# Four of sixteen gate projections computed with the values by Strassen's scheme, in a hybrid decoder layer on one core

## The chip, the cores and the metric

The kernel runs on 1 core of one Trainium2 chip. The metric is the device time of one execution in microseconds; the median of three runs before is 1684.72 us (1683.79 to 1685.11). The engines of the core, as the profile names them: PE is TensorE (matmuls, into banks of PSUM), DVE is VectorE, ACT is ScalarE, POOL is GpSimd, SP issues most transfers. Each of them works through its own instructions strictly in the order in which the program has them; semaphores make one wait for another.

## The reference, cut to what matters

One layer, x of 1024 rows x 1024 columns in float32. The part that the change touches is the combined projection of the normalised x and the use of its last 2048 columns, the gates.

```python
h = rms_norm(x, pre_mix_g[l])
proj = h @ w_in[l]
qa, ka, va, qb, kb, vb, gates = jnp.split(proj, split_at, axis=-1)
...
oa = diff_attention(qa, ka, va, lam)          # attention A: 4 heads, two softmaxes each, causal
...
    o_g, lse_g = dilated_group(qb[:, :, g], kb[:, :, g], vb[:, :, g], window, dil)   # attention B
...
g_a, g_b = jnp.split(jax.nn.sigmoid(gates), 2, axis=-1)
mix = (g_a * ya + g_b * yb) @ w_mix_out[l]
x = x + rms_norm(mix, post_mix_g[l])
```

After it comes a gated MLP with a convolution of three taps.

## The kernel before, in words

Every float32 product is made of three matmuls in a reduced format: each operand is split into a high part (a copy on ScalarE) and a rest (a subtraction on VectorE, L146), and `mm3` (L155 to L157) multiplies high by high, rest by high and high by rest. A matmul takes 128 x 128 weights and up to 512 moving columns. The stages are:

- **Values.** The 2048 value columns (512 of A, 1536 of B) are h times w_v. They are computed by Strassen's scheme on 2 x 2 blocks of 512: rows in two halves, the contraction in two halves of four 128-blocks, columns in halves. Seven products p1 to p7 replace eight; x enters as b11, b12, b21, b22 and the sums t2, t3, t4, the weights as blocks or sums of blocks. `steps_v` lists the steps in order, (product, column pair 0 or 1, k). `fetch_v` loads a step's weights 8 to 10 steps ahead, `ready_v` sums and splits them 5 steps ahead, `step_v` issues its 12 matmuls, and at a product's last k `take_v` moves the result from PSUM into the tiles y of the four quarters. The stores of the first columns' quarters, the norms of x, the angles and sines of the rotation are hung on step numbers (`STORE_AT`, `NORM_AT`, `TABLES_AT` and so on).
- **Attention A.** Four heads, each with eight blocks of 128 queries in the order 6, 7, 4, 5, 2, 3, 0, 1 (`attend_a`): scores (L784, L785) into two banks of PSUM, reduction with mask on VectorE (L787), exponentials on ScalarE (L794), ratio and combination of the two softmaxes on VectorE (L799 to L801); then, due one or two blocks later, transposes on TensorE (L713), split copies, products with the values (L725, L727), sums (L825, L826) and a norm by head (L857 to L866).
- **Attention B.** Twelve heads in three dilated groups, in the same manner with one softmax (`attend_b`).
- Merge, output projections with the gates, mix, up projection, down projection.

What fills TensorE beside the attention is projections: `proj_t` computes 128 columns for 1024 rows, 2 x 24 matmuls into one of three banks `acc`. A query or key projection is read from its bank by a rotation on ScalarE and VectorE (L700 to L703), a gate by one multiplication with the rows' norms (L250), after which it goes to a DRAM buffer `gt_d`. `interleave` spreads these fillers over the attention's steps by weight; `A_FILLS` gives them by head: p the next head's queries and keys (two projections), g a gate, v the transfer of the second pair of A's values, w their split, P, x and V the projections, transfer and value split of the first head of B. The framework then orders each engine's instructions by priority and readiness in a timeline of its own, so that fillers also move forward to where TensorE would stand; the position in the code doesn't settle the order.

Of the kernel before, what the change touches and what calls it, by code (L numbers as in the profile page):

```python
# [46 lines left out]
NH = NF // 2  # L47
AHEAD, T1_AT, LAST = 4, 5, 7
MIX_UNITS = {3: (0,), 4: (1,), 5: (2, 4), 6: (5,), 7: (6, 3, 7)}
START_GATES, A_FILLS, B_GATES = 1, ("gpgg", "gpvgg", "wgpgg", "xgPVgg"), 3  # L50
SLOTS = 18
LEFT_PAD = 48


XT_BUFS, NORM_AT, ANGLES_AT, SINES_AT, TABLES_AT, STORE_AT = 6, 14, 25, 33, 34, {35: 0, 36: 3, 39: 2, 41: 1}

K_FIRST = (4, 0, 5, 1, 6, 2, 7, 3)
RSQRT_MAGIC = float(0x5F3759DF)
# [29 lines left out]
def trunk(ctx: ExitStack, tc: tile.TileContext, a, out):  # L88
# [372 lines left out]
    with ExitStack() as st_y:  # L461
# [6 lines left out]
        def turns(pattern, *ps):  # L468

            ks = [iter(range(4)) for _ in ps]  # L470
            return [(ps[c], 1, next(ks[c])) for c in pattern]

        steps_v += [("p1", 1, k) for k in range(4)] + turns((0, 0, 1, 0, 1, 0, 1, 1), "p5", "p6")
        steps_v += turns((0, 0, 1, 1, 1, 1, 0, 0), "p3", "p7") + [("p4", 1, k) for k in range(4)]
        wz = [t[:, k % 2] for t in [wv.tile([P, 2, 512], F32, tag=f"wz{i}", name="wz") for i in range(2)] for k in range(2)]
        ready, got_v = {}, {}
# [10 lines left out]
        def new_y(name, pool=None):  # L487
            return [(pool or yv).tile([P, 512], F32, tag=f"y{name}{m}", name="yv") for m in range(4)]

        def fetch_v(n):  # L490
            p, i, k = steps_v[n]
            which = {"p1": ((0, 0),), "p2": ((0, 1),), "p5": ((1, 0), (1, 1)), "p6": ((0, 0),), "p7": ((0, 0), (1, 0)),
                     "p4": ((1, 1),), "p3": ((0, 1),)}[p]
            got_v[n] = [load_raw(a["w_v"][j * 4 + k][:, (2 * i + c) * 512 : (2 * i + c + 1) * 512], next(tags), parts=1 if n else 2)
                        for c, j in which]

        def ready_v(n, w=512):
            p, _, k = steps_v[n]
# [54 lines left out]
        quarter = {(0, i): new_y(f"a{i}") for i in range(2)}  # L553
        banks = {}

        def step_v(n):
            p, i, k = steps_v[n]
            x = xs_of[p]
            if p in ("p1", "p2", "p5") and k == 0:
                left = p == "p1"  # L560
                banks[left] = ([psum() for _ in range(3)] + [psum(F32, ps_o, "o")] if left else
                               [psum(F32, q, t) for q, t in ((ps_s, "s"), (pt, "pt")) for _ in range(2)])
            use = banks[p in ("p1", "p6", "p7", "p4")]
            wh, wl = ready.pop(n)
            for m in range(4):
                tk = slice(m * P, (m + 1) * P)
                mm3(use[m], x[0][:, k, tk], x[1][:, k, tk], wh, wl, k == 0 and p in ("p1", "p2", "p5"), k == 3, p in ("p6", "p7", "p4", "p3"))
            if k < 3:
                return
            with tc.high_priority(offset=80):  # L570
                for m in range(4):
                    take_v(p, i, m, use[m])
            if p == "p7" and i == 0:
                for m in range(4):
                    tt(quarter[3, 0][m], banks[False][m], quarter[3, 0][m], ALU.add)
# [56 lines left out]
        for n in range(8, len(steps_v)):  # L632
            p, i, k = steps_v[n]
            while fetched < min(n + (8 if n <= TABLES_AT else 10), len(steps_v)):
                fetch_v(fetched)
                fetched += 1
            while made < min(n + 5, len(steps_v)):
                ready_v(made)
                made += 1
            if 0 <= n - NORM_AT < 11:  # L640
                norm_x(n - NORM_AT)
            if n == NORM_AT + 11:
                lambda_scale()
            if n == TABLES_AT + 2:
                scale_tables(*args)
            if n == TABLES_AT + 4:
                tags = more_tags()
            if n == ANGLES_AT:
                pos = [load_raw(a["positions"][sl].partition_broadcast(P), next(tags)) for sl in halves()]
                args = [tb.tile([P, S], F32, tag=n_, name=n_) for n_ in ("sin", "cos")]  # L650
                angles(pos, *args, tb)
            if n in STORE_AT:
                put_v(STORE_AT[n], 0, True)
            if n == SINES_AT:
                make_sines(*args)
            if n == TABLES_AT:
                turn_norms()
            if k == 0 and (p, i) in places_y:
                q, name, pool = places_y[p, i]
                quarter[q, i] = new_y(name, pool)  # L660
            step_v(n)
            if k == 3 and i and p in ("p1", "p7", "p4", "p3"):
                put_v({"p1": 0, "p7": 3, "p4": 2, "p3": 1}[p], 1, p == "p1")
            if (p, i) == ("p5", 1):

                again.append(load_raw(a["xT"][k][:, 512:], next(tags)))
            if (p, i) == ("p6", 1):
                with behind_marks():
                    split_x(k, halves()[1], again[k])
# [199 lines left out]
        later(1, sums)  # L869
        later(3, norm)  # L870

    free_gates = list(range(2 * KC))

    def gates(n):

# [591 lines left out]
    def put(step, *srcs):  # L1467

        operands[step] = []
        for src in srcs:  # L1470
            operands[step].append(next(places)())
            split(*operands[step][-1], src)
# [329 lines left out]
```

## Time and profile before

| | |
|---|---|
| median of three runs | 1684.72 us |
| the profiled execution: time, span | 1684.85 us, 1683.1 us |
| TensorE busy, granted clock | 99%, 0.999 |
| VectorE, ScalarE, GpSimd busy | 78%, 54%, 10% |
| values' stage (up to the first score of attention A) | 0 to 204 us |
| attention A | 204 to about 500 us |
| attention B to the first output projection | about 500 to 865 us |

The profile has one execution on the chip. A record of an instruction has a start and a duration; matmuls overlap in their records, so that the distance between two starts is what one costs. The chain of waits, the waits by engine, groups of instructions and windows are views of the same trace. Their lines follow where the prediction uses them.

### The profile page before, as it was taken

Reading aid. Unit: us, or ns where it says so; the run is one execution under the profiler, and the core shown is the slowest. Engines: PE = TensorE matmul, PEld = TensorE weight load, DVE = VectorE, ACT = ScalarE, POOL = GpSimd, SP = SyncE. Lnnn points to the kernel's source line nnn. Section 1 sums busy time; section 2 is a strip of 40 time slices with the busy share of each in tenths; the row PEclk is TensorE's granted clock in tenths of the full one; section 3 lists DMA queues with packets and bytes.
Section 4 is the critical chain, followed back from the end, with each engine's and each line's share of the span. In section 5 each row is a group of like instructions: output and inputs, shape, how many; then the busy total and the mean of one; then the engine's idle time right before and its main releaser. Section 6 shows DMA issues by size and latency. Waiting matters only on the chain. (4 is left out here: it accounts for less than half of the span.)

```text
span 1683.1 us, 22937 instructions
## 1 busy us (share of the span) xinstructions
PE 1668.5 (99%) x7878; PEld 1394.0 (83%) x7878; DVE 1308.4 (78%) x2430; ACT 913.4 (54%) x1707; POOL 170.2 (10%) x267
## 2 busy tenths in 40 slices
PE   9999999999999999999999999999999999999997
PEld 7888888888888888888888888887888888888886
DVE  8795576877777777788766865988888778799978
ACT  7633574655445677667554533565554455255453
POOL 0031000000000000000123400022211121000000
PEclk9999999999999999999999999999999999999999
DMA  8767421315122212343676532267755655296524
GB/s 269 234 221 266 132 83 62 107 57 147 48 70 75 76 57 78 107 135 105 212 264 223 188 113 89 58 159 172 161 133 132 156 137 126 96 348 214 193 88 150
DMA packets 117253, 241.59 MB, mean 144 GB/s; under 512 B 14528, under 2 KB 23680, under 8 KB 117136
## 3 DMA queue, kind: packets, MB, share of 16 engines
q1 hardware_dynamic: 89296, 171.28, 30.6%
q0 software_dynamic: 23088, 60.45, 15.2%
q10 hardware_dynamic: 4752, 8.39, 1.3%
q8 instruction: 62, 1.02, 0.3%
q14 instruction: 55, 0.45, 0.1%
HBM read 177.54 MB, written 47.86 MB: 134 GB/s over the span
## 5 line engine op out<-in xcount | busy, mean ns | idle before, releaser
L157 PE MATMUL acc<-xl,whi 128*128 128x512 f32 x768 | 302.5, 394 | 0.0
L155 PE MATMUL acc<-xh,whi 128*128 128x512 f32 x768 | 302.0, 393 | 0.0
L156 PE MATMUL acc<-xh,wlo 128*128 128x512 f32 x768 | 301.7, 393 | 0.0
L149 ACT ACTIVATE whi<-raw 128x512 fp32r<-128x512 f32 (+1 forms) x249 | 154.1, 627 | 180.6 <-PE acc L157 115.4
L146 DVE TENSOR_TENSOR wlo<-raw,whi 128x512 fp32r<-128x512 f32 (+1 forms) x249 | 172.2, 700 | 32.8 <-ACT whi L149 27.9
L156 PEld LDWEIGHTS acc<-xh,wlo 128*128 128x128 f32 x768 | 144.4, 188 | 27.9
L157 PEld LDWEIGHTS acc<-xl,whi 128*128 128x128 f32 x768 | 144.4, 188 | 27.7
L155 PEld LDWEIGHTS acc<-xh,whi 128*128 128x128 f32 x768 | 144.5, 188 | 27.3
L155 PE MATMUL acc<-mh,whi 128*128 128x512 f32 x384 | 149.7, 390 | 1.7 <-ACT u L1447 1.3
L156 PE MATMUL acc<-mh,wlo 128*128 128x512 f32 x384 | 149.4, 389 | 0.0
L157 PE MATMUL acc<-ml,whi 128*128 128x512 f32 x384 | 149.1, 389 | 0.0
L700 ACT ACTIVATE t<-acc 64x512 f32<-64x512 f32 (+1 forms) x160 | 94.7, 592 | 62.0 <-PE acc L157 60.4
L149 ACT ACTIVATE whi<-s 128x512 fp32r<-128x512 f32 x80 | 49.8, 627 | 90.7 <-PE acc L157 63.5
L1443 DVE TENSOR_TENSOR u<-acc,u 128x512 f32<-128x512 f32 x100 | 68.5, 687 | 29.1 <-PE acc L157 28.9
L701 DVE TENSOR_TENSOR t<-acc,cos 128x512 f32<-128x512 f32 x64 | 44.2, 690 | 55.4 <-ACT t L700 51.9
L155 PEld LDWEIGHTS acc<-mh,whi 128*128 128x128 f32 x384 | 72.1, 188 | 17.7 <-ACT u L1447 2.2
L157 PEld LDWEIGHTS acc<-ml,whi 128*128 128x128 f32 x384 | 72.1, 188 | 14.9
L156 PEld LDWEIGHTS acc<-mh,wlo 128*128 128x128 f32 x384 | 72.1, 188 | 14.9
L1620 PE MATMUL acc<-whi,wlo 128*128 128x512 f32 x216 | 76.1, 390 | 0.0
L1619 PE MATMUL acc<-whi 128*128 128x512 f32 x216 | 74.8, 389 | 0.0
L1621 PE MATMUL acc<-wlo,whi 128*128 128x512 f32 x216 | 71.6, 390 | 0.0
L787 DVE CUSTOM_DVE_ANT_0 s<-s,mask_a 128x512 f32<-128x512 f32 (+3 forms) x96 | 52.5, 555 | 23.2 <-PE s L785 18.5
(402 smaller groups left out, 4015.2 us busy)
## 6 DMA issues: line engine op xcount, KB each, us to landing
raw<-in_w_in SPq DMA_DIRECT2D x96, 256.0 KB, 2.8
raw<-in_w_v SPq DMA_DIRECT2D x71, 256.0 KB, 4.6
raw<-in_w_up SPq DMA_DIRECT2D x68, 256.0 KB, 3.6
raw<-c_d SPq DMA_DIRECT2D x48, 256.0 KB, 3.6
c_d<-c SPq DMA_DIRECT2D x22, 512.0 KB, 4.0
s<-in_w_up POOLq DMA_DIRECT2D x40, 256.0 KB, 4.2
s<-s POOLq DMA_DIRECT2D x40, 256.0 KB, 3.9
raw<-in_w_down SPq DMA_DIRECT2D x37, 256.0 KB, 3.5
```

Of the source, the lines that this page charges most:

```text
L146: eng.tensor_tensor(lo, src, hi.bitcast(F32), op=ALU.subtract)
L149: copy = nc.scalar.activation(hi, src, AF.Copy)
L155: nc.tensor.matmul(o, sh, mh, start=first, stop=False, skip_group_check=on)
L156: nc.tensor.matmul(o, sl, mh, start=False, stop=False, skip_group_check=on)
L157: nc.tensor.matmul(o, sh, ml, start=False, stop=last, skip_group_check=on)
L700: nc.scalar.activation(t1[dst], ps[src], AF.Copy)
L701: nc.vector.tensor_tensor(t2, ps, cos[:, sl], op=ALU.mult)
L787: nc.vector.tensor_tensor_reduce(out=s_sb[:, c0:c1], in0=ps, in1=mask, scale=-scale, scalar=3.0e38, op0=ALU.add, op1=ALU.min, accum_out=mx ...
L1443: nc.vector.tensor_tensor(to, made(p), x, op=ALU.add)
L1619: nc.tensor.matmul(banks[m], gh[:, tk], wh, start=f == 0, stop=False)
L1620: nc.tensor.matmul(banks[m], gl[:, tk], wh, start=False, stop=False)
L1621: nc.tensor.matmul(banks[m], gh[:, tk], wl, start=False, stop=f == NH - 1)
```

## The change

Four of the sixteen gates (numbers 12 to 15) are no longer fillers. They form two pairs of 256 columns, and each pair is computed in the values' stage by the same seven products: rows and contraction are halved as for the values, the two gates of a pair are the two column halves. The fourteen new steps stand between p1 of the second columns and p5, p6. As in a gate before, the gate's 128 columns stay in the array and 512 rows of x move; as in the value steps, sums of blocks are formed on VectorE first. Results go to `gt_d` from POOL's queue instead of ScalarE's. The lists of fillers lose one gate a head. The split of the second pair of A's values (w) goes from the start of head 2 to the end of head 1. The stores of the first value quarters get other step numbers.

```diff
-START_GATES, A_FILLS, B_GATES = 1, ("gpgg", "gpvgg", "wgpgg", "xgPVgg"), 3
+PAIRS, START_GATES, A_FILLS, B_GATES = 2, 1, ("gpg", "gpvgw", "gpg", "xgPVg"), 3
...
-XT_BUFS, NORM_AT, ANGLES_AT, SINES_AT, TABLES_AT, STORE_AT = 6, 14, 25, 33, 34, {35: 0, 36: 3, 39: 2, 41: 1}
+XT_BUFS, NORM_AT, ANGLES_AT, SINES_AT, TABLES_AT, STORE_AT = 6, 14, 25, 33, 34, {32: 0, 37: 3, 42: 2, 46: 1}
...
-        steps_v += [("p1", 1, k) for k in range(4)] + turns((0, 0, 1, 0, 1, 0, 1, 1), "p5", "p6")
+        steps_v += [("p1", 1, k) for k in range(4)]
+        steps_v += [(p, "gate", x) for p in ("p2", "p1", "p5", "p6", "p7", "p4", "p3") for x in range(PAIRS)]
+        steps_v += turns((0, 0, 1, 0, 1, 0, 1, 1), "p5", "p6")
...
+            if i == "gate":
+                srcs = [w_in[where[GT + gate_of(k, c) * P]][:, j * 512 : (j + 1) * 512] for c, j in which]
...
+        def take_gate(p, n, use):
+            def put(q):
+                sl = halves()[q % 2]
+                y = gate_y[n][q]
+                tt(y, use if p == "p4" else y, rstd_row[:, sl], ALU.mult)
+                nc.gpsimd.dma_start(gt_d[gate_of(n, q // 2)][:, sl], y)
+            y = gate_y[n]
+            if p in ("p2", "p6", "p7"):
+                nc.scalar.activation(y[{"p2": 0, "p6": 1, "p7": 3}[p]], use, AF.Copy)
+            if p == "p1":
+                tt(y[0], use, y[0], ALU.add)
+                put(0)
+            if p == "p7":
+                tt(y[3], banks[n, False], y[3], ALU.add)
+                put(3)
+            if p == "p4":
+                put(2)
+            if p == "p3":
+                tt(y[1], use, y[1], ALU.add)
+                put(1)
+        def step_gate(p, n, wh, wl):
+            left = p in ("p1", "p6", "p7", "p4")
+            if p in ("p1", "p2"):
+                banks[n, left] = psum(F32, pt, "pt") if left else psum(F32, ps_s, "s")
+            x, use = xs_of[p], banks[n, left]
+            for k in range(4):
+                c = slice(k * P, (k + 1) * P)
+                mm3(use, wh[:, c], wl[:, c], x[0][:, k], x[1][:, k], k == 0 and p in ("p1", "p2", "p5"), k == 3, p in ("p6", "p7", "p4", "p3"))
+            with tc.high_priority(offset=80):
+                take_gate(p, n, use)
...
+            if (p, i, k) == ("p2", "gate", 0):
+                ya, yb = new_y("a0"), new_y("b3", yw)
+                gate_y.update({x: {0: ya[x], 1: ya[2 + x], 3: yb[x], 2: yb[2 + x]} for x in range(PAIRS)})
...
-    free_gates = list(range(2 * KC))
+    free_gates = list(range(2 * (KC - PAIRS)))
```

How the order of the instructions moves shows at three places. Lines after L460 or so carry higher numbers in the changed kernel (L784 is L835, L713 is L764, L725 is L776).

**Place 1, TensorE at the end of head 3 of attention A**, around the scores of the last query block (`s<-k,a` and `s<-k,b` are scores, `pt<-ident,s` transposes, `o<-pt,vh` products with values, `acc<-xh,whi` a projection). Before:

```order
L713 MATMUL pt<-ident,s 128x128
L784 MATMUL s<-k_3716,a_3712 128x256
L785 MATMUL s<-k_3716,b_3714 128x256
L156 MATMUL acc<-xh,wlo 128x512
L713 MATMUL pt<-ident,s 128x128 x5
L157 MATMUL acc<-xl,whi 128x512
L155 MATMUL acc<-xh,whi 128x512
L156 MATMUL acc<-xh,wlo 128x512
L157 MATMUL acc<-xl,whi 128x512
```

In the changed kernel:

```order
L776 MATMUL o<-pt,vh 128x512
L776 MATMUL o<-pt,vh 128x2x128
L778 MATMUL o<-pt,vl 128x128
L778 MATMUL o<-pt,vl 128x256
L764 MATMUL pt<-ident,s 128x128
L835 MATMUL s<-k_3890,a_3886 128x256
L836 MATMUL s<-k_3890,b_3888 128x256
L764 MATMUL pt<-ident,s 128x128 x5
L835 MATMUL s<-k_3891,a_3887 128x256
L836 MATMUL s<-k_3891,b_3889 128x256
L155 MATMUL s<-kh,qh 128x128
L156 MATMUL s<-kh,ql 128x128
```

The projections that stood between these matmuls are gone from here; no matmul into `acc` stands among the 67 from the scores of query block 2 to the last values.

**Place 2, TensorE in the first head of attention B** (`s<-kh,qh` scores, `pt<-ident,bs` transposes). Before:

```order
L157 MATMUL acc<-xl,whi 128x512
L155 MATMUL acc<-xh,whi 128x512
L156 MATMUL acc<-xh,wlo 128x512
L157 MATMUL acc<-xl,whi 128x512
L725 MATMUL o<-pt,vh 128x512
L725 MATMUL o<-pt,vh 128x2x128 x2
L727 MATMUL o<-pt,vl 128x128 x2
L727 MATMUL o<-pt,vl 128x256
L713 MATMUL pt<-ident,bs 128x128 x3
L155 MATMUL s<-kh,qh 128x256
L156 MATMUL s<-kh,ql 128x256
L157 MATMUL s<-kl,qh 128x256
```

In the changed kernel:

```order
L155 MATMUL s<-kh,qh 128x256
L156 MATMUL s<-kh,ql 128x256
L157 MATMUL s<-kl,qh 128x256
L776 MATMUL o<-pt,vh 128x512
L776 MATMUL o<-pt,vh 128x2x128 x2
L778 MATMUL o<-pt,vl 128x128 x2
L778 MATMUL o<-pt,vl 128x256
L1101 MATMUL pt<-ident,stat 16x128
L764 MATMUL pt<-ident,bs 128x128 x4
L776 MATMUL o<-pt,vh 128x512
L776 MATMUL o<-pt,vh 128x2x128 x2
L778 MATMUL o<-pt,vl 128x128 x2
```

Here too the projections have moved ahead; the head's scores, transposes and values follow each other directly.

**Place 3, VectorE at the end of head 3** (`vl<-vperm` is the value split of B's first pair, `ql<-t` the split of B's queries, `t<-acc,cos` the first read of a projection's bank). Before:

```order
L146 TENSOR_TENSOR vl<-vperm,vh 128x1024
L826 TENSOR_TENSOR osb<-osb,o 128x256
L146 TENSOR_TENSOR vl<-vperm,vh 128x1024
L146 TENSOR_TENSOR pt<-pt 128x512
L787 ISA s,mx<-s,mask_a 128x256
L787 ISA mx 128x1
L146 TENSOR_TENSOR pt<-pt 128x384
L146 TENSOR_TENSOR wlo<-raw,whi 128x512
L250 TENSOR_TENSOR gate<-acc,rstd_row 128x512
L146 TENSOR_TENSOR wlo<-raw,whi 128x512
```

In the changed kernel:

```order
L176 TENSOR_TENSOR rhw<-rhw,rhv 128x4
L146 TENSOR_TENSOR vl<-vperm,vh 128x1024
L177 SCALAR_TENSOR_TENSOR rhy<-rhw,rhy 128x4
L146 TENSOR_TENSOR vl<-vperm,vh 128x1024
L877 TENSOR_TENSOR osb<-osb,o 128x256
L175 TENSOR_TENSOR rhw<-rhy 128x4
L947 TENSOR_TENSOR ql<-t_5152,qh 128x512
L947 TENSOR_TENSOR ql<-t_5213,qh 128x512
L176 TENSOR_TENSOR rhw<-rhw,rhv 128x4
L752 TENSOR_TENSOR t_5288<-acc,cos 128x512
L752 TENSOR_TENSOR t_5351<-acc,cos 128x512
```

The value split now stands behind the last softmaxes instead of between them, and the projection's banks are read only after it.

More of the change, by code (lines that the diff above doesn't have):

```diff
@@ L488, in new_y, with gate_of @@
             return [(pool or yv).tile([P, 512], F32, tag=f"y{name}{m}", name="yv") for m in range(4)]
+        def gate_of(x, c):
+            return 2 * (KC - PAIRS + x) + c
         def fetch_v(n):
@@ L493, in fetch_v @@
                      "p4": ((1, 1),), "p3": ((0, 1),)}[p]
-            got_v[n] = [load_raw(a["w_v"][j * 4 + k][:, (2 * i + c) * 512 : (2 * i + c + 1) * 512], next(tags), parts=1 if n else 2)
-                        for c, j in which]
+            if i == "gate":
+                srcs = [w_in[where[GT + gate_of(k, c) * P]][:, j * 512 : (j + 1) * 512] for c, j in which]
+            else:
+                srcs = [a["w_v"][j * 4 + k][:, (2 * i + c) * 512 : (2 * i + c + 1) * 512] for c, j in which]
+            got_v[n] = [load_raw(src, next(tags), parts=1 if n else 2) for src in srcs]
         def ready_v(n, w=512):
@@ L554, in trunk @@
         banks = {}
+        gate_y = {}
+        def take_gate(p, n, use):
[28 more added lines that the diff above has]
+                take_gate(p, n, use)
         def step_v(n):
             p, i, k = steps_v[n]
+            if i == "gate":
+                step_gate(p, k, *ready.pop(n))
+                return
             x = xs_of[p]
```

## The prediction

> **What bounds the kernel now.** The first lines of the profile's page and the waits of TensorE come first.
>
> ```profile
> span 1683.1 us, 22937 instructions
> ...
> PE 1668.5 (99%) x7878; PEld 1394.0 (83%) x7878; DVE 1308.4 (78%) x2430; ACT 913.4 (54%) x1707; POOL 170.2 (10%) x267
> ```
> ```profile
> engine line waited for: us in total, times, longest us
> PE acc L155 <- ACT xh L387: 1.4, 1, 1.4
> PE acc L155 <- DVE ya L1211: 1.4, 2, 0.9
> PE acc L155 <- ACT u L1447: 1.3, 1, 1.3
> ```
>
> TensorE is busy 99% of the span, and its longest wait is 1.4 us. Nothing else sets the end, so time goes only by matmuls left out, and comes only by new waits of TensorE. A matmul's duration in the records (0.39) isn't its price, since matmuls overlap; the timeline of TensorE gives that by its starts.
>
> ```profile
> 1324.20 0.39 PE L155 MATMUL acc<-mh,whi 128*128 128x512 f32 x1
> ...
> 1326.92 0.39 PE L155 MATMUL acc<-t4h,whi 128*128 128x512 f32 x1
> ```
> ```profile
> 541.02 0.28 PE L156 MATMUL s<-kh,ql 128*128 128x256 f32 x1
> 541.14 0.28 PE L157 MATMUL s<-kl,qh 128*128 128x256 f32 x1
> ```
> ```profile
> 491.86 0.71 PE L713 MATMUL pt<-ident,s 128*128 128x128 f32 x5
> 492.32 0.48 PE L157 MATMUL acc<-xl,whi 128*128 128x512 f32 x1
> ```
>
> Twelve matmuls of 512 columns start within 2.72 us, 0.227 each; one of 256 columns costs 0.12, and a transpose of 128 some 0.1 (five within 0.46).
>
> How much cover the attention has shows in the windows of head 3 (426 to 500 us) and of the passage to attention B.
>
> ```profile
> core 0: us, PE busy (x) PEld busy (x) DVE busy (x) ACT busy (x) POOL busy (x), PEclk, DMA share, GB/s
> ...
> 426.00:500.00 74.00, 74.00 (x382) 62.74 (x381) 55.66 (x152) 36.21 (x80) 0.00 (x0) 1.00 0.18 60
> 500.00:530.00 30.00, 30.00 (x150) 25.32 (x150) 19.26 (x50) 11.62 (x21) 1.14 (x4) 1.00 0.28 91
> ```
>
> VectorE is 75% busy in the head and 64% after it. TensorE doesn't wait there because projections and gates stand between the attention's matmuls.
>
> **Term 1: matmuls that go.** A gate is 2 halves x 8 k x 3 = 48 matmuls of 512, four are 192. The seven products for two pairs are 2 x 7 x 4 k x 3 = 168. The built programs agree: 6732 matmuls of 512 columns become 6708, all other sizes keep their number. 24 x 0.227 = **-5.45 us**.
>
> Two windows of the values' stage as it is now (the columns are those above: VectorE third, transfers last) show the room there.
>
> ```profile
> 120.00:130.00 10.00, 10.00 (x45) 8.27 (x45) 9.02 (x16) 5.84 (x10) 5.04 (x9) 1.00 1.03 380
> 130.00:140.00 10.00, 10.00 (x46) 8.26 (x45) 4.67 (x7) 3.58 (x6) 0.00 (x0) 1.00 0.96 334
> ```
>
> What the gates add in the values' stage (14 splits, 8 sums of two weights, 14 passes over PSUM or the sums) is 36 VectorE instructions of 0.6, 22 us beside 38 us of new matmuls, and 20 copies on ScalarE, 12 us. VectorE has room there (4.67 of 10 us busy from 130 to 140 us), and the steps keep five splits of lead, so I cost it at nothing; without that cover it would be the 22 us. The stores of the first values only change places among POOL's transfers, and the gates' stores go from ScalarE's queue to POOL's; what all these transfers may do is rival 4. The second value split goes from the start of head 2 to the end of head 1: two ScalarE and two VectorE instructions between the same neighbours, its two transfers where they were, at nothing; the most it could cost is its own two copies and subtractions, some 4 us, if TensorE stood for all of them.
>
> **Term 2: cover that goes.** Each head of attention A loses one gate, 48 x 0.227 = 10.9 us of matmuls that wait for no attention. The order of the changed program shows where it is missing. Heads 0 to 2 still mix projections in. At the end of head 3, after the scores of query block 2 and up to the last values of block 1, 67 matmuls follow each other with no projection among them (places 1 and 3 in the section on the change). TensorE works in order, so whatever waits there holds all that is queued behind it, and it can go only as fast as VectorE hands on: scores are reduced there before their banks come free, and the projection that ends the stretch waits for a bank that VectorE has to read. VectorE's prices, again by starts:
>
> ```profile
> 481.31 0.69 DVE L146 TENSOR_TENSOR pt<-pt 128x512 fp32r<-128x512 f32 x1
> 481.91 0.68 DVE L250 TENSOR_TENSOR gate<-acc,rstd_row 128x512 f32<-128x512 f32 x1
> 482.51 0.68 DVE L146 TENSOR_TENSOR wlo<-raw,whi 128x512 fp32r<-128x512 f32 x1
> ...
> 491.25 0.16 DVE L799 RECIPROCAL rc<-den 128x1 f32<-128x1 f32 x1 [0.56 <-ACT s L794]
> 491.45 0.22 DVE L800 SCALAR_TENSOR_TENSOR ratio<-rc,den,nlam 128x1 f32<-128x1 f32 x1
> 491.70 0.35 DVE L801 SCALAR_TENSOR_TENSOR s<-s,ratio 128x128 f32<-128x128 f32 x1
> ...
> 492.55 1.22 DVE L146 TENSOR_TENSOR vl<-vperm,vh 128x1024 fp32r<-128x1024 f32 x1
> 493.69 0.41 DVE L826 TENSOR_TENSOR osb<-osb,o 128x256 f32<-128x256 f32 x1
> ```
> ```profile
> L146 DVE TENSOR_TENSOR pt<-pt 128x384 fp32r<-128x384 f32 x6 | 3.3, 552 | 0.0
> ...
> L787 DVE CUSTOM_DVE_ANT_0 s<-s,mask_a 128x384 f32<-128x384 f32 x4 | 2.1, 556 | 1.3 <-PE s L785 1.2
> ...
> L787 DVE CUSTOM_DVE_ANT_0 s<-s,mask_a 128x256 f32<-128x256 f32 x4 | 1.7, 420 | 0.1
> ...
> L787 DVE CUSTOM_DVE_ANT_0 s<-s,mask_a 128x128 f32<-128x128 f32 x4 | 1.2, 290 | 1.1 <-PE s L785 1.1
> ...
> L801 DVE SCALAR_TENSOR_TENSOR s<-s,ratio 128x768 f32<-128x768 f32 x1 | 1.0, 1021 | 0.0
> L801 DVE SCALAR_TENSOR_TENSOR s<-s,ratio 128x256 f32<-128x256 f32 x2 | 1.0, 482 | 0.0
> ...
> L801 DVE SCALAR_TENSOR_TENSOR s<-s,ratio 128x512 f32<-128x512 f32 x1 | 0.7, 746 | 0.0
> ```
>
> An instruction of 512 elements lasts 0.69 but the next starts after 0.60, so I take 0.085 off each duration. In the changed order VectorE works between the scores that begin the dry stretch and the read of the projection's bank that ends it: reductions of scores 2 x 512, 2 x 384, 2 x 256, 2 x 128 (3.2 us); subtractions 3 x 512, 2 x 384 (2.7); combinations of the two softmaxes 768, 512, 384, 256, 128 (2.8); three sums of 256 (1.0); the two halves of B's value split (2.3); three of 512 for B's projection (1.8); some 17 small ones (1.6): 15.4 us. TensorE's side is 12 x 0.227 + 2 x 0.18 + 23 x 0.12 + 30 x 0.1 = 8.8 us. **So TensorE waits at least 6.6 us.** This is a floor: VectorE itself waits for exponentials and copies on ScalarE that no projection covers now.
>
> ```profile
> L149 ACT ACTIVATE pt<-pt 128x512 fp32r<-128x512 f32 x7 | 3.9, 593 | 1.8 <-PE pt L713 1.7
> ...
> L149 ACT ACTIVATE vh<-vperm 128x1024 fp32r<-128x1024 f32 x2 | 2.1, 1046 | 0.0
> ...
> L794 ACT ACTIVATE s<-s,mx 128x512 f32<-128x512 f32 x2 | 1.4, 716 | 0.0
> ...
> L794 ACT ACTIVATE s<-s,mx 128x256 f32<-128x256 f32 x2 | 1.0, 504 | 0.0
> ```
>
> Following the stretch instruction by instruction with these rows, VectorE stands still about 0.9 us for the first transposes and their copy, 0.3 + 0.2 + 0.2 for pairs of exponentials, 0.3 for the last scores, 0.2 for the value copies of 1.05 us, and a reciprocal, ratio and combination that hang on each other take 0.45 where I counted 0.2 (0.5 in all): 2.6. Term 2 is 6.6 + 2.6 = **+9.2 us**.
>
> **Term 3: a second dry stretch.** The projections that were to stand beside the first head of attention B were used up while VectorE caught up (between the two stretches the order has 35 us of projections). B's first head then runs without them (place 2). In its last part TensorE has 20 x 0.12 + 3 x 0.227 + 23 x 0.1 = 5.4 us.
>
> ```profile
> L1028 DVE TENSOR_TENSOR osb<-osb,o 128x256 f32<-128x256 f32 x14 | 7.1, 504 | 1.7 <-ACT osb L1027 1.7
> ...
> L896 DVE TENSOR_TENSOR kl<-t,kh 128x512 fp32r<-128x512 f32 x6 | 6.6, 1108 | 1.5 <-ACT kh L895 1.5
> ```
>
> VectorE has four reductions of 256 (1.3), three sums (1.3), subtractions of 512, 384 and 512 (1.7), the next value split (2.3), two key splits with strides (2.0) and one of 512: 9.2 us, 3.8 more. ScalarE's two value copies of 1.05 us ahead of small copies that TensorE needs add some 1.1. **+4.9 us.**
>
> **Sum.** The profiled execution took 1684.85 us (span 1683.1, 1.75 around it), 0.13 above the median of the three runs. 1684.85 - 5.45 + 9.2 + 4.9 = **1693.5 us**.
>
> [...]
>
> **Rivals.**
> 1. The forecast: both stretches starve TensorE. For it: the counts above, and VectorE's 75% with the cover still there. Chance 0.67.
> 2. The cover holds: VectorE and ScalarE run far enough ahead, so that no stretch starves. This is one mechanism, a lead of VectorE at the start of a dry stretch; it decides where the lead exceeds 6.6 + 2.6 us. But VectorE cannot lead, since its first reduction needs TensorE's scores from the same stretch. 1684.85 - 5.45 = 1679.4, faster by 0.32%. Chance 0.07.
> 3. Half: only the plain load of one stretch shows, 3.8 to 6.6 us: 1683 to 1686, within 0.2%. Chance 0.13.
> 4. Transfers in the values' stage starve TensorE as well. The windows under term 1 show the queues nearly full (380 and 334 GB/s). The gates' 38 us bring 18 loads and 8 stores of 0.26 MB beside 16 stores of values and 1.6 MB of tables, 12.6 MB. At 380 GB/s that is 33 us, at 334 it is 38 us: hidden, but with nothing to spare. If a tenth of it comes late, TensorE waits 3 us more: 1696.5; twice that is the upper end, 1699. Chance 0.13.
>
> A clock that falls would add to the same end: TensorE would wait about 4 us in one piece at the end of the first dry stretch. The windows show 1.00 throughout, with no wait over 1.5 us to test it. [...]
>
> That the change doesn't do what it says is excluded by the count of 24.
>
> **How the numbers follow.** 0.2% (3.4 us) is about what a measurement of this kernel tells from no change: 1681.5 to 1688.2. Faster is rival 2; same is rival 3; slower is 1 and 4. The range goes from the floors of both stretches less half the shorter one (1684.85 - 5.45 + 6.6 + 1.9 = 1687.9) to rival 4's end, 1699; rivals 2 and 3 lie outside, 0.2 together.
>
> ```profile
> 203.69 0.39 PE L784 MATMUL s<-k,a 128*128 128x512 f32 x1
> ```
>
> **What would show it.** The row above is the first score of attention A. Right: TensorE waits in the profile after add up to some 14 us, two thirds of it between about 508 and 530 us for VectorE's scores, softmaxes and the projection's bank, the rest between about 560 and 580; that score comes 168 x 0.227 = 38 us later (at 242 instead of 204 us); windows of the up projection are unchanged. Wrong: no wait of TensorE above 1 us in these stretches (rival 2), or waits for split weights between 105 and 150 us (rival 4).

## The result, and the profile after

The changed kernel takes **1701.26 us** (median of four runs, 1698.67 to 1703.40) beside 1684.76 of the kernel before, a ratio of **1.0097** (95% interval 1.0082 to 1.0112): 16.5 us slower. The direction was forecast, the size was not: +8.8 us were forecast and 1699 was the upper end of the range. The profiled execution took 1700.62 us, 15.77 more than that of before. Two executions on record, one of the kernel before (4345.69 us) and one of e18 (2326.59 us), fell in a slow state and are in no ratio here.

The page and the waits of TensorE in the profile after:

```profile
span 1698.8 us, 22947 instructions
...
PE 1673.5 (99%) x7854; PEld 1395.1 (82%) x7854; DVE 1318.6 (78%) x2450; ACT 919.8 (54%) x1719; POOL 172.7 (10%) x275
```
```profile
engine line waited for: us in total, times, longest us
PE acc L155 <- DVE t L752: 3.9, 1, 3.9
PE o L776 <- DVE osb L1079: 3.8, 2, 3.2
PE pt L764 <- DVE s L852: 1.8, 2, 1.3
PE acc L155 <- ACT xh L387: 1.3, 1, 1.3
PE pt L764 <- ACT rows L1102: 1.3, 1, 1.3
```

The 24 matmuls are gone (7878 to 7854), and four of these five rows are new. The timeline of TensorE in the same profile has the first score of attention A and the longest wait:

```profile
242.03 0.39 PE L835 MATMUL s<-k,a 128*128 128x512 f32 x1
...
530.95 0.80 PE L155 MATMUL acc<-xh,whi 128*128 128x512 f32 x1 [3.94 <-DVE t L752]
531.55 0.63 PE L156 MATMUL acc<-xh,wlo 128*128 128x512 f32 x1
531.97 0.63 PE L157 MATMUL acc<-xl,whi 128*128 128x512 f32 x1
532.40 0.63 PE L155 MATMUL acc<-xh,whi 128*128 128x512 f32 x1
```
```profile
530.00:540.00 10.00, 9.05 (x31) 7.26 (x32) 8.41 (x19) 5.26 (x8) 0.00 (x0) 0.71 0.08 27
...
580.00:600.00 20.00, 19.93 (x105) 17.00 (x104) 19.36 (x43) 15.69 (x34) 0.00 (x0) 0.91 0.29 93
...
860.00:870.00 10.00, 6.79 (x22) 5.26 (x21) 2.83 (x6) 6.44 (x10) 0.85 (x1) 0.67 0.80 295
```

The first score comes at 242 us, 38 later than before, as forecast. After a wait of 3.94 us the matmuls start 0.427 apart in place of 0.227: the windows (the second block, columns as in the prediction) show a granted clock of 0.71 there, of 0.91 from 580 to 600 us, and of 0.67 at a place that the forecast did not have, 860 to 870 us. In the trace's clock record these are, ahead of the end of the run, three spells at half speed, from 528.88, 580.08 and 863.38 us, 6.83, 3.41 and 6.83 us long.

To see where the time went, I took each distance between two starts of TensorE, subtracted what such a matmul costs (0.227, 0.176, 0.12 or 0.11 us for 512, 384, 256 or 128 columns), and summed what was left over where it was more than 0.06. The text below calls such a sum a wait; matmuls made late by a halved clock are in it. "End of A" is the 25 us on either side of attention A's last score, "first head of B" the 60 us behind that, "end of B" reaches from 12 us before attention B's last score to 75 us behind it. For before and after, and for the experiments told below (in us):

| kernel | profiled | values | end of A | first head of B | end of B |
|---|---|---|---|---|---|
| before | 1684.85 | 0.1 | 0.6 | 1.0 | 2.4 |
| e13, before again | 1683.64 | 0.1 | 0.6 | 1.0 | 2.8 |
| after | 1700.62 | 0.5 | 11.9 | 5.6 | 7.2 |
| e5, after again | 1704.86 | 5.1 | 12.9 | 6.8 | 6.6 |
| e1, before with less cover | 1701.24 | 0.1 | 11.3 | 6.0 | 3.0 |
| e2, three gates in head 3 | 1699.56 | 2.9 | 7.8 | 6.7 | 7.7 |
| e3, one pair | 1695.17 | 8.1 | 0.9 | 5.8 | 3.9 |
| e7, one pair, twelve in A | 1701.38 | 9.9 | 0.6 | 1.0 | 4.3 |
| e6, two pairs, twelve in A | 1705.69 | 0.8 | 0.6 | 1.0 | 20.4 |
| e9, split earlier | 1698.66 | 0.5 | 17.6 | 0.8 | 5.0 |
| e14, late merge | 1695.18 | 1.6 | 12.1 | 6.6 | 0.5 |
| e16, start gate to B | 1695.87 | 1.8 | 11.3 | 5.6 | 2.5 |

(In e9 the waits begin earlier, and the 10.2 us ahead of the 25 are counted in. A row is one execution: e3's profiled one lies 4.4 us below its median, e5's 4.4 above.) From before to after: -5.45 for the matmuls, +0.4, +11.3, +4.6 and +4.8 make **+15.7**, beside the 15.77 measured; all the rest differs by 0.1 us in sum.

The halved clock has its part in three of these numbers. Behind the wait at 530.95 nine matmuls of 512 columns start 0.2 us late each, 1.8 us; behind the one at 863.93 ten do, 2.0 us; from 580.08 to 583.49 TensorE is busy throughout at half speed, which makes up to 1.7 us. Together that is up to 5.5 of the 15.7 us. A window of 100 us in the up projection holds the same 443 matmuls, first before, then after:

```profile
1200.00:1300.00 100.00, 100.00 (x443) 82.81 (x442) 79.25 (x100) 53.48 (x77) 19.70 (x33) 1.00 0.61 140
```
```profile
1216.00:1316.00 100.00, 100.00 (x443) 82.81 (x442) 79.22 (x101) 52.90 (x77) 19.19 (x32) 1.00 0.60 138
```

### The profile page after: what moved, and what is told of

The parts are those of the page before. It is cut to its first block, busy times and chain, and to the rows that moved or that the text cites. A ratio compares the mean times of both kernels' runs of the same rounds, so it can differ in the third digit from the quotient of the medians.

```text
span 1698.8 us, 22947 instructions
## 1 busy us (share of the span) xinstructions
PE 1673.5 (99%) x7854; PEld 1395.1 (82%) x7854; DVE 1318.6 (78%) x2450; ACT 919.8 (54%) x1719; POOL 172.7 (10%) x275
## 5 line engine op out<-in xcount | busy, mean ns | idle before, releaser
L155 PE MATMUL acc<-xh,whi 128*128 128x512 f32 x704 | 278.4, 396 | 3.9 <-DVE t L752 3.9
L157 PE MATMUL acc<-xl,whi 128*128 128x512 f32 x704 | 278.8, 396 | 0.0
L156 PE MATMUL acc<-xh,wlo 128*128 128x512 f32 x704 | 278.6, 396 | 0.0
L155 PEld LDWEIGHTS acc<-xh,whi 128*128 128x128 f32 x704 | 133.3, 189 | 30.0 <-DVE t L752 4.3
L156 PEld LDWEIGHTS acc<-xh,wlo 128*128 128x128 f32 x704 | 133.3, 189 | 26.3
L157 PEld LDWEIGHTS acc<-xl,whi 128*128 128x128 f32 x704 | 133.5, 190 | 25.9
```

Of the source, the lines that this page charges most:

```text
L155: nc.tensor.matmul(o, sh, mh, start=first, stop=False, skip_group_check=on)
L156: nc.tensor.matmul(o, sl, mh, start=False, stop=False, skip_group_check=on)
L157: nc.tensor.matmul(o, sh, ml, start=False, stop=last, skip_group_check=on)
```

## Experiments

The theory at this point: the gates that left the heads of attention A cost the time, as cover, whatever makes them. The rival: the seven products, with their transfers and sums, cost it where they stand. A second question came with the wait near 864 us.

### Is it the cover or Strassen's scheme? (e1, e4, e2, e3)

e1: the kernel before, four gates more ahead of attention A, the lists as in the changed kernel.

```diff
-START_GATES, A_FILLS, B_GATES = 1, ("gpgg", "gpvgg", "wgpgg", "xgPVgg"), 3
+START_GATES, A_FILLS, B_GATES = 5, ("gpg", "gpvgw", "gpg", "xgPVg"), 3
```

> The kernel before, without Strassen's scheme for any gate: four plain gates more ahead of attention A, two gates in each of its heads as in the changed kernel. All the work is kept, only the cover is placed as in the changed kernel. Theory (the missing gates in the heads cost the time): the same two dry stretches wait as in the changed kernel, 11.9 + 5.3 us, and the third wait near the end of attention B may or may not show (up to 4.4): 1684.8 + 17.2 = 1702.0, to 1706.4 with the third. Rival (the seven products, their transfers or their sums cost it): no stretch waits, 1684.8.

Measured: 1701.47 us, ratio 1.0102 (1.0087 to 1.0117), as the theory had it. The stretches wait 11.3 and 6.0 us, as in the changed kernel, with the same longest wait in the view of waits of e1:

```profile
PE acc L155 <- DVE t L701: 3.9, 1, 3.9
```

Not one gate is made by Strassen's scheme here, and all the work of before is done. **The placing of the cover alone costs what the change costs there.** That e1 is no slower than the changed kernel, though it has 24 matmuls more, is the end of B (3.0 in place of 7.2 us), taken up below.

e4: the kernel before with the second value split alone moved.

```diff
-... ("gpgg", "gpvgg", "wgpgg", "xgPVgg"), 3
+... ("gpgg", "gpvggw", "gpgg", "xgPVgg"), 3
```

> The kernel before with the second value split of attention A moved alone, from the start of head 2 to the end of head 1. Both theories: no difference, 1684.8 within 1 us. If more than 3 us come, the move is a cause of its own.

Measured: 1687.88 us, ratio 1.0019 (1.0009 to 1.0028), 1.5 to 4.7 us slower. Both theories missed. The two stretches wait as little as before (0.7 and 1.2 us); the end of B waits 4.7 in place of 2.4. This doesn't simply add to the rest: e1 has the same move, and its end of B waits 3.0.

e2: the changed kernel, the gate ahead of attention A put into head 3. e3: one pair by Strassen's scheme, ten gates in the heads.

```diff
-PAIRS, START_GATES, A_FILLS, B_GATES = 2, 1, ("gpg", "gpvgw", "gpg", "xgPVg"), 3
+PAIRS, START_GATES, A_FILLS, B_GATES = 2, 0, ("gpg", "gpvgw", "gpg", "xgPVgg"), 3
+PAIRS, START_GATES, A_FILLS, B_GATES = 1, 1, ("gpg", "gpvgg", "wgpg", "xgPVgg"), 3
```

> The changed kernel with the gate that stood ahead of attention A put into its head 3, which then has three as before. Theory: both stretches lose their waits (11.9 + 5.3 us), 1701.3 - 17.2 = 1684.1, and 1679.7 if the third wait near the end of attention B goes too; what the gate ahead of attention A covered there is unknown, 0 to 5 us more. Rival (seven products): stays at 1701. Rival (the second stretch is short of cover by itself, not because its projections were used up early): only the first goes, 1689.4.

> Two gates by Strassen's scheme in place of four; 14 gates are left, and heads 1 and 3 of attention A keep three of them, heads 0 and 2 have two. The second value split stays at the start of head 2. Theory: 12 matmuls fewer, -2.7 us, head 3 has its cover and no stretch waits: 1682.1; with the third wait 1686.5. Rival (seven products cost by themselves, half as much here): 1684.8 + 8 = 1693.

Measured: 1697.51 us (ratio 1.0074, 1.0052 to 1.0095) and 1699.58 us (1.0087, 1.0066 to 1.0107). Neither gate in head 3 brought what I expected: the end of A still waits 7.8 us in e2, and in e3, where it is clean, the first head of B waits 5.8. So it isn't head 3's own list that counts. Both stretches together wait 1.6 us with twelve gates in attention A (before), 6.7 with ten (e3), 14.5 with nine (e2), 17.3 to 19.7 with eight (e1, after, e5). So the cover acts as one pool: the program's order draws fillers forward, and what is short is mostly short at the end. e3's values' stage waits 8.1 us as well. One pair means seven steps fewer there, while the stores keep the step numbers set for two pairs; whether that is why was not tried.

### Twelve gates in attention A (e6, e7)

```diff
-PAIRS, START_GATES, A_FILLS, B_GATES = 2, 1, ("gpg", "gpvgw", "gpg", "xgPVg"), 3
+PAIRS, START_GATES, A_FILLS, B_GATES = 2, 0, ("gpgg", "gpvgg", "wgpgg", "xgPVgg"), 0
+PAIRS, START_GATES, A_FILLS, B_GATES = 1, 0, ("gpgg", "gpvgg", "wgpgg", "xgPVgg"), 2
```

> Four gates by Strassen's scheme, but all twelve that are left stand in the heads of attention A, three in each as before; none ahead of it and none in the last head of attention B. Theory (cover in attention A is one pool, and 12 gates are enough, 10 leave 5.5 us of waits in the second stretch): both stretches are as clean as before (0.6 + 1.0 us). The last head of attention B loses 33 us of matmuls as cover; if it is like the first head of B it waits 5 to 6 us more, 1684.8 - 5.5 + 5.5 = 1684.8; if the projection of attention A's output that follows it serves as cover, 1679.4. The rival (the seven products cost by themselves) says 1690 or more.

> Two gates by Strassen's scheme; twelve of the 14 that are left stand in the heads of attention A, none ahead of it, two in the last head of attention B. Theory: both stretches clean, -2.7 us, the end of attention B with one gate less: 1682.1 to 1685. If the values' stage waits for its transfers as with one pair before (8.1 us), 1690.

Measured: 1701.77 us (ratio 1.0106, 1.0084 to 1.0127) and 1699.81 us (1.0090, 1.0071 to 1.0109). Both are slower than the theories had them (1684.8 at most for e6, 1690 for e7), and by its time alone e6 would fit the rival; where the time is lost decides. Windows of e6 over the two stretches:

```profile
500.00:530.00 30.00, 30.00 (x164) 25.78 (x163) 20.74 (x58) 13.63 (x37) 0.00 (x0) 1.00 0.24 80
530.00:540.00 10.00, 10.00 (x51) 8.43 (x50) 5.49 (x12) 3.87 (x8) 0.90 (x4) 1.00 0.12 39
...
580.00:600.00 20.00, 20.00 (x112) 17.35 (x111) 16.93 (x33) 15.69 (x32) 0.00 (x0) 1.00 0.13 40
```

TensorE is busy throughout: with four gates by Strassen's scheme and twelve in attention A both stretches are as clean as before, and the values' stage waits 0.8 us, which settles the first question. But the waits come back where the other gates were taken from, in the view of waits of e6:

```profile
PE acc L155 <- ACT oah L149: 3.8, 2, 3.3
PE acc L155 <- ACT obh L149: 3.7, 1, 3.7
PE acc L155 <- DVE gl L1294: 2.9, 1, 2.9
PE o L776 <- DVE osb L1079: 2.9, 1, 2.9
```

The end of B, without its three gates, waits 20.4 us where I expected 0 to 6 more than before, and 3 us stand just ahead of it. Here too a lower clock is in the sum: windows of e6 show a granted clock of 0.74 from 842 to 862 us and of 0.83 from 862 to 882 us. In e7, with one gate less there, it waits 4.3 us, the values' stage 9.9 with a single pair, and the second output projection 5.3.

### What sets the first dry stretch? (e9, e10, e11, e12, e15)

The prediction put it down to VectorE's load. Five runs tried that. e9 moved the split of B's first values ahead of the projection:

```diff
-... "xgPVg"), 3
+... "xgVPg"), 3
```

> The changed kernel with the split of attention B's first values ahead of the projection in head 3's cover, so that its 2.3 us of VectorE and 2.1 us of ScalarE no longer fall in the dry stretch. Theory (VectorE's load sets that stretch, and the 4.1 us wait in one piece costs a halved clock on top): its waits go from 11.9-12.9 to 7 to 9 us, the longest to under 2 us, and the matmuls 0.427 apart behind it vanish; 1701.0 - 4 = 1697. Rival (the chain of scores, exponentials, transposes and sums sets it whatever else VectorE does): 11.9 and 4.1 again.

Measured: 1701.13 us, ratio 1.0099 (1.0079 to 1.0120), no gain. The instructions moved with it: a window of e9 shows the waits 30 us earlier, and none at 530 or in the first head of B.

```profile
460.00:500.00 40.00, 29.71 (x146) 22.91 (x145) 32.88 (x110) 21.24 (x50) 0.00 (x0) 0.88 0.05 19
500.00:530.00 30.00, 30.00 (x158) 25.50 (x157) 22.72 (x61) 14.36 (x34) 0.91 (x4) 0.99 0.21 67
```

The sum stayed: 17.6 + 0.8 us, beside 17.5 in the profile after. This fits one pool of cover; for VectorE's load it decides nothing. e10 to e12 gave the subtractions of the splits to GpSimd, in head 3 and the first head of B (e10), in all of attention A (e11), and that in the kernel before (e12):

```diff
-                split(hi[:, sl], lo[:, sl], raw)
+                split(hi[:, sl], lo[:, sl], raw, lo_on[0])
...
-                split(*res[-1], v)
+                split(*res[-1], v, lo_on[0])
...
+            lo_on[0] = nc.gpsimd if h >= 3 else None
```

> The changed kernel with the subtractions of all weight and value splits in head 3 of attention A and in the first head of attention B on GpSimd, which stands idle there (1.54 us for 512 elements in the profile against VectorE's 0.60). In the first dry stretch VectorE loses 2.3 + 1.8 of its 15.4 us, in the second 2.3 of 9.2. Theory: 11.9-12.9 becomes 7 to 8, 5.6-6.8 becomes 3 to 4; 1701.0 - 7 = 1694. Rival (the chain): no change; a second (GpSimd's slowness is a new wait for split weights): up to 5 us more.

> As the run before this one, in all heads of attention A and the first of attention B: VectorE loses 2.4 us for each projection or gate of 10.9 us of matmuls. Theory (cover is used up along the whole attention because VectorE falls behind, and what is left at its end is what is short): both stretches lose most of their waits (17.5-19.7 us to 2 to 8), 1701.0 - 13 = 1688, at best 1683. Rival: the order of the instructions alone sets the waits, 1694 as with head 3 alone; or GpSimd is too slow, 1701 or more.

> The kernel before with the same subtractions on GpSimd in all of attention A and the first head of attention B. It has no waits there to lose: 1684.8 within 2 us. If it is slower by more, GpSimd's pace costs by itself, and that is to be taken off in the run before this one.

Measured: 1702.90 us (ratio 1.0107, 1.0090 to 1.0124), 1707.69 us (1.0132, 1.0110 to 1.0153) and 1688.41 us (1.0017, 1.0008 to 1.0027): e11 is slower than the changed kernel and e12 slower than the kernel before, e10 can't be told from the changed kernel, and none gained. The timeline of GpSimd, VectorE and TensorE in e10 shows why:

```profile
526.81 4.67 POOL L148 TENSOR_TENSOR vl<-vperm,vh 128x1024 fp32r<-128x1024 f32 x2 [66.85 <-ACT vh L151]
...
526.93 2.26 DVE L179 SCALAR_TENSOR_TENSOR rhy<-rhw,rhy 128x4 f32<-128x4 f32 x1
529.23 2.26 DVE L177 TENSOR_TENSOR rhw<-rhy 128x4 f32<-128x4 f32 x1
531.53 0.16 DVE L178 TENSOR_TENSOR rhw<-rhw,rhv 128x4 f32<-128x4 f32 x1
...
534.42 0.80 PE L157 MATMUL acc<-xh,whi 128*128 128x512 f32 x1 [6.76 <-DVE t L754]
```

While GpSimd makes two subtractions of 2.3 us, two of VectorE's instructions of four elements, 0.16 us otherwise, last 2.26 each. VectorE was not relieved: these two held it for 4.5 us where its own two subtractions took 2.3, and TensorE's wait grew from 3.9 to 6.8. Unmeant, this is an experiment with more load. e15 made it cleanly, with VectorE's two subtractions made twice:

```diff
-                split(*res[-1], v)
+                split(*res[-1], v), [sub(nc.vector, res[-1][1], v, res[-1][0]) for _ in range(wk_b == [] and len(ops_b[steps[0]]) > 0)]
```

> The changed kernel with VectorE's two subtractions of the split that falls in the first dry stretch made twice: 2.3 us more of VectorE there, nothing else. Theory (VectorE's load sets that stretch): the wait of 4.1 us becomes 6.4, 1701 + 2.3 = 1703.3. Rival (a chain through several engines sets it): 4.1 again, 1701.

Measured: 1705.64 us, ratio 1.0117 (1.0100 to 1.0133), 4.4 us above the changed kernel where 2.3 were expected; in the profile the values' stage waits 3.9 us besides. The wait, in e15's timeline:

```profile
537.35 0.80 PE L155 MATMUL acc<-xh,whi 128*128 128x512 f32 x1 [6.20 <-DVE t L752]
```

6.20 in place of 3.94, 2.26 more for the 2.3 added. **In that part of the stretch VectorE's load sets TensorE's wait one for one.** That less load shortens it was not shown: no run took load away without moving the order.

### The end of attention B (e5, e8, e13, e14, e16, e17)

The wait at 863.93 us in the profile after, with what stands ahead of it on ScalarE and VectorE; then ScalarE at the same place before:

```profile
861.66 1.06 ACT L1240 ACTIVATE gl<-gl 128x1024 f32<-128x1024 f32 x1 [2.98 <-DMA gl<-gt_d]
862.62 0.61 ACT L1078 ACTIVATE osb<-o 128x256 f32<-128x256 f32 x1
...
863.26 0.62 DVE L1079 TENSOR_TENSOR osb<-osb,o 128x256 f32<-128x256 f32 x1 [3.79 <-ACT osb L1078]
...
863.93 0.58 PE L776 MATMUL o<-pt,vh 128*128 128x256 f32 x1 [3.21 <-DVE osb L1079]
```
```profile
846.98 1.06 ACT L1189 ACTIVATE gl<-gl 128x1024 f32<-128x1024 f32 x1 [0.45 <-DMA gl<-gt_d]
847.94 0.64 ACT L1027 ACTIVATE osb<-o 128x256 f32<-128x256 f32 x1
```

TensorE needs bank o back. Its reader on ScalarE could go, but is queued behind a sigmoid that waits for its gate's load: 0.45 us before, 2.98 now. The instructions stand in the same order in both kernels here. Six runs asked whether this belongs to the change:

```diff
 e8
-                    side(gts[-1], gt_d[first + len(gts) - 1])
+                    (side if first else dma)(gts[-1], gt_d[first + len(gts) - 1])
 e14: as e8, and
-    for i, fn in zip((1, 2, 3, 5, 9), merge(2, ob)):
+    for i, fn in zip((1, 2, 3, 7, 10), merge(2, ob)):
-    for i, fn in zip((3, 5, 7, 11, 16), merge(BH - 1, ob)):
+    for i, fn in zip((3, 5, 6, 13, 16), merge(BH - 1, ob)):
 e16
+PAIRS, START_GATES, A_FILLS, B_GATES = 2, 0, ("gpg", "gpvgw", "gpg", "xgPVg"), 4
 e17
-            return 2 * (KC - PAIRS + x) + c
+            return 8 + 2 * x + c
-    free_gates = list(range(2 * (KC - PAIRS)))
+    free_gates = [i for i in range(2 * KC) if not 8 <= i < 12]
```

> The changed kernel a second time, nothing altered. The two dry stretches are set by the order of the program: 11.9 and 5.6 us again, within 0.5. The wait near the end of attention B (7.2 us there against 2.4 before) hangs on when transfers land: if that is so, it comes out anywhere from 2 to 8 us, and the values' stage may show a wait for a transfer too; the rival, that it belongs to the change as the dry stretches do, says 7.2 again. Time 1696 to 1703.

Measured: 1700.44 us, ratio 1.0097 (1.0073 to 1.0120). The two stretches wait 12.9 and 6.8 us, each about 1 more than in the profile after, where I had allowed 0.5. The clock has a part in the first: e5's windows show 0.94 from 500 to 530 us and 0.75 from 530 to 540, those of the profile after 0.98 and 0.71, 4.3 us lost in these 40 beside 3.5. The end of B waits 6.6 us, 1.8 of it at the place shown for the profile after and most of the rest at three others, the last of them in this timeline (line numbers are one higher than in the changed kernel):

```profile
913.74 1.76 DVE L1159 TENSOR_TENSOR mw<-og,mw 128x1536 f32<-128x1536 f32 x1 [6.34 <-DMA mw<-e_d]
...
916.02 0.68 DVE L1263 TENSOR_TENSOR ya<-acc,gl 128x512 f32<-128x512 f32 x1
...
916.76 0.50 PE L156 MATMUL acc<-oah,whi 128*128 128x512 f32 x1 [1.70 <-DVE ya L1263]
```

It is the same pattern on VectorE: the reader of TensorE's bank stands behind a merge product that waits for a load. And in the values' stage, clean in the profile after, e5 waits 5.1 us:

```profile
131.02 0.63 ACT L150 ACTIVATE whi<-raw 128x512 fp32r<-128x512 f32 x1 [7.70 <-DMA raw<-in_w_in]
131.55 0.58 ACT L577 ACTIVATE yv<-pt 128x512 f32<-128x512 f32 x1
...
132.19 0.72 PE L156 MATMUL pt<-t3h,whi 128*128 128x512 f32 x1 [3.11 <-ACT yv L577]
```

ScalarE waits 7.7 us for a gate's weights, with the copy that frees the bank behind it.

> The changed kernel with the loads of the first branch's gates issued from SyncE's queue in place of GpSimd's, where four of them stood behind the store of the merge's weights. Theory (the wait near the end of attention B is ScalarE's sigmoid waiting for such a load, with the copy of the value sums queued behind it): that wait goes, 7.2 becomes 2 to 3 us, 1701.3 - 4.5 = 1696.8; the dry stretches stay at 11.9 and 5.6. Rival (the end of attention B is short of cover like the stretches): no change there.

Measured: 1699.63 us, ratio 1.0088 (1.0064 to 1.0111). The wait of 3.2 us is gone, but 4.3 us stay, most of it for the merge products.

> The kernel before a second time, nothing altered, for its waits near the end of attention B. Theory (those hang on when transfers land): they come out between 2 and 6 us in place of 2.4, and the time at 1684 to 1688; the rival (the changed cover makes them long) says 2.4 again.

Measured: 1685.21 us, ratio 0.9999 (0.9990 to 1.0009); 2.8 us. That is the foot of the theory's range and nearer to the rival's 2.4. The profiles on hand speak against a draw from 2 to 6 us in every kernel: 2.4 and 2.8 for the kernel before, 7.2, 6.6 and (e17 below) 6.4 for the changed order. The cover in attention A alone doesn't decide it, since e1 waits 3.0.

> The changed kernel with the loads of the first branch's gates on SyncE's queue, and VectorE's two merge products near the end of attention B placed two jobs later, so that no read of a PSUM bank is queued behind a product that waits for a load. Theory: 6.6-7.2 us of waits there become 2 to 3; the dry stretches (about 18 together) stay; 1701 - 4.5 = 1696.5. Rival (short of cover): 4 to 7 us stay.

Measured: **1692.53 us**, ratio 1.0046 (1.0031 to 1.0061). In the view of waits of e14 no row for a merge or a gate's load is left:

```profile
PE acc L155 <- DVE t L752: 3.9, 1, 3.9
PE acc L155 <- ACT xh L387: 2.0, 2, 1.4
PE pt L764 <- DVE s L852: 1.8, 2, 1.3
```

The end of B waits 0.5 us, the stretches as ever (12.1 and 6.6). The median fell by 8.7 us where 4.5 were expected; the profiled execution, with 1695.18 the longest of its four, fell by 5.4: the end of B gave 6.7, the values' stage and the first head of B took 2.1 back.

> The changed kernel with the gate that stands ahead of attention A put into the last head of attention B, which then has four. Theory: the dry stretches stay (18), the gate was no cover where it stood, the end of attention B has 10.9 us more of matmuls over the same transfers and loses 2 to 4 of its 6.6-7.2 us: 1698. Rival (those waits are for transfers at fixed places, no cover reaches them): 1701; if the gate was cover ahead of attention A, 1703.

Measured: 1697.18 us, ratio 1.0073 (1.0057 to 1.0088). The end of B waits 2.5 us, and nothing but the wait for a gate's weights that e5 has in the values' stage too (1.8 us in all there) stands ahead of attention A: there the gate was no cover, here it is.

> The changed kernel with the same order of instructions on every engine, but Strassen's scheme makes gates 8 to 11 in place of 12 to 15, so that the last head of attention B makes 13 to 15 as in the kernel before, into the same rows of memory as there. Theory (the later landing of loads near the end of attention B has to do with where the gates lie in memory): 6.6-7.2 us of waits there become 2.4 to 3, 1697. Rival (it has to do with what the cores' queues do at that time, not with addresses): 5 to 8 us, 1701.

Measured: 1699.42 us, ratio 1.0085 (1.0071 to 1.0100), 6.4 us at the end of B: where the gates lie in memory is not the reason. Followed back, a lag begins some 26 us earlier, where ScalarE's copy into osb waits for the store of the osb before it. One row each of before, after and e1:

```profile
823.21 0.68 ACT L1027 ACTIVATE osb<-o 128x256 f32<-128x256 f32 x1 [1.16 <-DMA og_d<-osb]
```
```profile
835.66 0.70 ACT L1078 ACTIVATE osb<-o 128x256 f32<-128x256 f32 x1 [2.61 <-DMA og_d<-osb]
```
```profile
840.06 0.66 ACT L1027 ACTIVATE osb<-o 128x256 f32<-128x256 f32 x1 [2.16 <-DMA og_d<-osb]
```

The four gate loads on GpSimd's queue, before and after:

```profile
841.35 2.17 POOL L1187 DMA_DIRECT2D gl<-gt_d  x4
```
```profile
853.50 2.16 POOL L1238 DMA_DIRECT2D gl<-gt_d  x4
```

Counted from attention B's last score (838.98 and 849.99 us), these loads and the three of merge weights behind them are issued 0.95 to 1.35 us later in the profile after and in e17 than before, 0.3 to 0.4 later in e1. That is only part of it. The load that the sigmoid waits for lands 3.7 us later in the profile after than before, 1.1 by its issue and 2.5 because it takes 8.1 us to land in place of 5.6 (6.5 in e5, 5.9 in e17, 5.0 in e1). Why the store and this load take longer in the changed programs, I could not settle.

### A version faster than both (e18)

The two edits of e14 in the kernel before:

> The kernel before with the two edits of the late-merge run: gate loads of the first branch on SyncE's queue and the merge products two jobs later. Theory (bank reads are no longer queued behind an instruction that waits for a load): the 2.4 to 2.8 us of waits near the end of attention B become under 0.6, 1684.9 - 2.1 = 1682.8, faster than both kernels, at the edge of what can be told. Rival (the edits only help where loads land late): 1684.9.

Measured: **1682.78 us** beside 1684.91, ratio 0.9988 (0.9979 to 0.9997). All waits of TensorE that its view lists for e18:

```profile
engine line waited for: us in total, times, longest us
PE acc L155 <- ACT xh L387: 2.4, 2, 1.4
PE pt L594 <- DVE t4l L591: 1.2, 1, 1.2
PE acc L155 <- ACT mh L149: 0.3, 1, 0.3
```

The end of B waits 0.9 us in place of 2.4. It is faster than both kernels, by about as much as was expected; the gain is small, but the whole interval lies below 1.

## Why the prediction was right in direction and half in size

- **Term 1, -5.45 us: right by the count.** The attention begins 5.2 us earlier in the changed kernel (242.03) than in e1, which makes the same four gates plainly ahead of it; the first score of e1:

```profile
247.24 0.39 PE L784 MATMUL s<-k,a 128*128 128x512 f32 x1
```

- **Values' stage at nothing: right in the profile after (+0.4 us), not in every execution** (e5 5.1, e15 3.9). Rival 4 had the right place. In e5 the wait reached TensorE through ScalarE, which stood for a late load with the copy of a bank queued behind it; whether the volume made the load late is not shown.
- **Moved split at nothing: wrong, +3.1 us by itself** (e4), and not where its own instructions stand: the end of B waited 2.3 us longer in e4's profile. Why is open.
- **Term 2, +9.2 us: right but for the clock.** Measured 11.3. Nine matmuls behind the long wait start 0.2 us late each, 1.8 us; without them it is 9.5. The prediction names a falling clock beside its sum ("would add to the same end") and has no term for it; with no wait over 1.5 us and a clock of 1.00 in its windows, the profile before gave nothing to size one by.
- **Term 3, +4.9 us: the total is right (4.6), by luck in part.** Up to 1.7 us of it are the halved clock from 580.08 us on, so that the waits themselves come to about 2.9: the term was too large by 2, and a clock that nobody had forecast there filled it up. Its reason was wrong too: "used up while VectorE caught up". In e3 the first stretch does not wait and the second still does; in e6, with twelve gates in attention A, neither does. The pool is short as a whole.
- **The sum: two terms were missing.** The steps that failed are these. First, a sum that ends at 580 us takes for granted that what stands in the same order behind the passage costs the same; the end of B took 4.8 us more, 2.8 without the clock. The trace of before showed the thin margin (0.45 us for a load, 0.9 for a merge), and I did not ask what a later phase of the transfers would do to it. Second, the sum has no term for the halved clock; in all it made up to 5.5 us. With the 2 us that term 3 had too much, these explain the 7.1 us between the forecast and the profile within 1 us.
- **With both kernels' ends of B cured, the forecast comes near.** e14 beside e18 is 1692.53 beside 1682.78, 9.75 us, where the three terms say 8.65. This holds for the medians; e14's profiled execution, the longest of its four, lies 14.0 above e18's, so that it is no close test of the terms.
- Rival 2 (cover holds) and rival 3 (half) fell. At the end of the first stretch VectorE had no lead: work added to it there came out as TensorE's wait in full (e15).

## What to carry to other kernels

Leaving out a filler's matmuls saves what they cost, but a filler can be worth more than that where it hides another engine. In this kernel a gate by Strassen's scheme saves 24 x 0.227 / 4 = 1.4 us, and taken out of attention A it cost 2.6 to 4.5 us of waits (5.1 us more for two gates less, 15.7 to 18.1 for four), out of the last head of B 2 to 6 (1.9 for one in e7, 18 for three in e6), halved clock included. Count cover by stage and over the whole stage, not by the list of one head, since a scheduler draws fillers forward and the lack shows at the end. Where an instruction that waits for a load stands ahead of one that frees a PSUM bank, its margin was the kernel's margin here (0.45 us before; 3.21 us of TensorE's wait after, where the sigmoid waited 2.98 us for its load): put the bank's reader first, as e14 and e18 do.

## What the hardware showed that I had not expected

**A halved clock after waits of 1.3 to 7 us.** In the profile after, nine starts of 512 columns stand 0.427 us apart behind the wait of 3.94 us that ends at 530.95, and ten behind the one of 3.21 us that ends at 863.93, where 0.227 is the cost otherwise. In e10 a wait of 6.76 us has a granted clock of 0.57 behind it (534 to 540 us), and in e2 starts are 0.43 apart behind one of 1.83 us that ends at 908.49. The length of one wait doesn't decide it. In the profile after, the spell at half speed from 580.08 us comes with a wait of 1.33 us that ends at 579.80, with one of 0.61 at 577.28 ahead of it. In the profile before, waits of 1.39 us (to 25.60) and 1.30 us (to 1151.34) have a granted clock of 1.00 around them (24 to 28 and 1148 to 1158 us), and so have two of 1.27 and 0.53 us, to 515.02 and 516.98, in the profile after (512 to 524 us). What does decide it was not shown.

**GpSimd held some of VectorE's instructions up, and not others.** In e10 two subtractions of 1024 elements on GpSimd, 2.3 us each, stretched two of VectorE's instructions of 4 elements from 0.16 to 2.26 us: work given to GpSimd was not taken off VectorE there. Other instructions kept their time: in the profile after, GpSimd makes four multiplications of 512 elements (L1295) from 930.00 us on, 6.51 us in all, and beside them a subtraction of VectorE (`wlo<-raw,whi`, at 930.43) takes 1.42 us where 0.69 is usual, but two multiplications of VectorE (`gl<-acc,gl`, from 931.77) take their usual 0.68 us each.
